# A hybrid decoder block on one core: expert blocks multiplied in pairs, and every indexed transfer an add

## The chip, the core and the metric

One core of a Trainium2 chip runs the whole program in one launch. The metric is the device time of one execution in microseconds (us). The kernel before was timed three times: 976.51, 976.25 and 974.28 us, median 976.25. One execution was profiled.

## The reference, cut to what matters

The layer takes 256 tokens of 1024 numbers. Two attention branches run side by side on the normed tokens (a block-sparse one, which with 256 tokens is plain causal attention, and a latent one), are merged by sigmoid gates, projected and added to the tokens. A channel mixer follows, and a last norm. The mixer is the part that the change touches. For each token and each of 8 heads it scores two sets of 128 sub-keys, keeps the best 16 of each, forms sums of pairs and keeps the best 16 of these. An expert is a pair of sub-keys, one of 128 x 128 = 16384. The softmax of a token's 16 best sums are its gates g, and the mixer adds up, over heads and picks,

    g * gelu(u_e . x) * v_e

where u_e and v_e are rows of two matrices of 16384 x 1024 and e is the picked expert. All of it is in float32, and the kernel has to keep that accuracy.

## The kernel before, in words

The kernel does not gather rows. It multiplies the normed tokens with all 16384 rows of u, takes the gelu of each product, multiplies these with a matrix of gates that is zero except at the picks, and multiplies the result with all rows of v. So the mixer is three streams: 16 query blocks, 128 blocks of u (128 experts each, 512 KB), 128 blocks of v.

A float32 number is kept as two parts, hi and lo, that TensorE multiplies at its fast float32 rate, and a product of two numbers is hi x hi + hi x lo + lo x hi. Each 512 KB unit of weights is loaded by SP into one of four `raw` buffers, copied into `hi` by ScalarE (L142) and subtracted into `lo` by VectorE (L146; GpSimd does this for some early units). `wget` (L155) emits the split of the units up to two ahead of the one that is used, and `emit_split` (L130) the load of the units up to three ahead of the one that it splits. There are four buffers each of `raw`, `hi` and `lo`. Every engine and every queue works in the order in which the program emits its instructions; Tile adds the semaphores.

The normed tokens stand in `h2`, for each of 8 groups of 128 channels hi and lo side by side, 256 tokens each. The first ten blocks of u, and the last four, are narrow (`u_mm`, L836): 24 products of 256 columns. Blocks 10 to 123 are wide (`u_wide`, L852): eight products of 512 columns, hi of the weight with hi and lo of the tokens at once (L857), then eight of 256, lo of the weight with hi of the tokens (L859). The sums need a PSUM bank each; blocks take two banks named `tr` and two named `sc` in twos (blocks 10 and 11 `tr`, 12 and 13 `sc`, and so on), so a bank is wanted again four blocks later.

A wide block is drained while the next one runs. `u_block` (L871) emits `u_sum` of the block before (ScalarE copies the right half, L864; VectorE adds the left half, L865), then what is handed in as `between`, then the new block's products, then `gelu_in` of the block before (L822): ScalarE writes the gelus of tokens 0 to 127 into the big buffer `gm` (L823), and those of tokens 128 to 255 into a small buffer `gs` (L828), which SP stores to the tensor `gld` in memory, one block later (`spill`, L815, L818).

The gates take two ways, one for each half of the tokens.

- Tokens 0 to 127: GpSimd writes them into a tensor `gd` of 128 x 128 x 128 zeros in memory, at addresses that each partition has in a register tile: 128 indexed transfers of 128 numbers each (`post`, L995, L1002), in eight groups of 16, one group for each head. A group may not begin before the one before it has landed. The first group writes plainly, the seven others add to what is there.
- Tokens 128 to 255: for each pair of tokens (a step q of 64) VectorE makes one-hot rows (`onehots`, L1096; L1100, L1102, two buffers each), ScalarE and VectorE weigh one set with the gates (`weigh`, L1105; L1112, L1113), TensorE multiplies them (`scatter`, L1115; two products of 256 columns, L1119), and ScalarE and VectorE put the result into `gm` (`place`, L1121; L1124, L1125). The loop at L1136 does one step with one block of u, and one block more after every third step. Step q makes the one-hots of step q + 2 and weighs those of step q + 1 (`pair`, L1132).

In the stage before that loop VectorE also finds and decodes the picks (`find`, L1016, `read`, L1026), one block of u at each yield. Between block 36 and 37 TensorE transposes the decoded indices and gates (`index_T`, L1073, `gate_T`, L1080).

After block 123 the pools of the one-hots, of `us` and of `gs` are closed (L1143 to L1146), a new pool takes their place, and SP loads gates and stored gelus back two blocks at a time (`reload`, L1156), for VectorE to multiply them into `gm` (`a_mult`, L1165), and ScalarE and VectorE to split (`a_split`, L1174). Each reload waits for the last group of indexed transfers (`ends`). The V stage then multiplies `gm` with the blocks of v: per block twelve products of 512 columns (L1194), with a scheme of fewer products for some pairs of half blocks (`w_mm`, L1270).

Of the kernel before, what the change touches and what calls it, by code (L numbers as in the profile page):

```python
# [11 lines left out]
F32 = mybir.dt.float32  # L12
# [5 lines left out]
OP = mybir.AluOpType  # L18
AX = mybir.AxisListType

P = 128
T = 256
NT = 2
D = 1024
ND = 8
# [19 lines left out]
def block_kernel(ctx, tc, consts, constb, pos, x, g_mix, g_ffn, g_fin, w_in, g_q, w_qup, g_kv, w_kvup,  # L45
                 w_ba, w_bb, w_out, w_pq, keys, exp_u, exp_v, out):
    nc = tc.nc
    V, S, G, PE = nc.vector, nc.scalar, nc.gpsimd, nc.tensor
# [6 lines left out]
    def acc():  # L55
        return ps.tile([P, 512], F32, name="acc", tag="acc", bufs=4)

    def sct():
        return ps.tile([P, 512], F32, name="sc", tag="sc", bufs=2)

    def trt():
        return ps.tile([P, 512], F32, name="tr", tag="tr", bufs=2)
# [22 lines left out]
    for dq in range(2):  # L85
        for hf in range(2):
            for u in range(2):
                k = 4 * hf + 2 * dq + u
# [66 lines left out]
    def wget(i, ahead=2):  # L155
        while state["split"] <= min(i + ahead, state["end"] - 1):
            emit_split()
        return split.pop(i)
# [14 lines left out]
    h2h, h2l = h2[:, :, 0], h2[:, :, 1]  # L173
    x2d = dram.tile([T, D], F32, name="x2d")
    gd = dram.tile([P * P * P, 1], F32, name="gd")
    gld = dram.tile([P, P, P], F32, name="gld")
# [348 lines left out]
    for hf in range(2):  # L525
        tiles = [acc(), acc()]
        hi, lo = wget(U_QUP[hf])
# [10 lines left out]
    hi, lo = wget(U_KVUP[0])  # L538
# [266 lines left out]
    gate = [gs.tile([P, 64], F32, name=f"gate{g}") for g in range(2)]  # L805
# [6 lines left out]
    T0, T1 = slice(0, P), slice(P, T)  # L812
    held = []

    def spill():  # L815
        while held:
            k, g = held.pop()
            nc.sync.dma_start(gld[k], g)  # L818

    vpool = []  # L820

    def gelu_in(j, so, keep=False):  # L822
        S.activation(gm[:, j, T0], so[:, T0], AF.Gelu)  # L823
        if keep:
            gl = vpool[0].tile([P, 2, T], F32, name="gl", tag="rl", bufs=3)[:, 0, :P]
        else:
            gl = gs.tile([P, P], F32, name="gs", bufs=3)
        S.activation(gl, so[:, T1], AF.Gelu)  # L828
        if keep:
            V.tensor_tensor(gm[:, j, T1], gm[:, j, T1], gl, op=OP.mult)  # L830
        else:
            spill()
            held.append((j, gl))


# [13 lines left out]
        gelu_in(j, u_mm(j), keep)  # L849


    def u_wide(j):  # L852
        hi, lo = wget(U_U[j])

        s = trt() if j & 2 else sct()
        for b in range(ND):
            PE.matmul(s, hi[:, b * P:(b + 1) * P], h2[:, b].rearrange("p z n -> p (z n)"), start=b == 0, stop=False)  # L857
        for b in range(ND):
            PE.matmul(s[:, :T], lo[:, b * P:(b + 1) * P], h2h[:, b, :], start=False, stop=b == ND - 1)  # L859
        return s  # L860

    def u_sum(s):
        u = gp.tile([P, T], F32, name="us", tag="us", bufs=3)
        S.activation(u, s[:, T:], AF.Copy)  # L864
        V.tensor_tensor(u, u, s[:, :T], op=OP.add)  # L865
        return u


    pend = []

    def u_block(j, keep=False, between=None):  # L871
        u = u_sum(pend[0][1]) if pend else None
        if between:
            between()
        new = j, u_wide(j)
        if pend:
            gelu_in(pend.pop()[0], u, keep)
        pend.append(new)

    def u_end(keep=False):  # L880
        j, s = pend.pop()
        gelu_in(j, u_sum(s), keep)


    qs = {}
# [109 lines left out]
    def post(g):  # L995


        for h in range(HG):
            own = []
            for k in range(16):  # L1000
                c = slice(16 * h + k, 16 * h + k + 1)
                i = nc.gpsimd.indirect_dma_start(  # L1002
                    out=gd[:, :], out_offset=bass.IndirectOffsetOnAxis(ap=addr[g][:, c], axis=0),
                    in_=gate[g][:, c], in_offset=None, compute_op=OP.add if g or h else OP.bypass).ins
                nc.gpsimd.nop()
                for m in own:
                    tc.declare_no_dep(i, m, reason="other experts")
                if k == 0:
                    for m in ends:
                        tc.add_manual_dep(i, m.name, SYNC, reason="same tokens, next head")  # L1010
                own.append(i)
            ends[:] = own
# [41 lines left out]
    done = [0]  # L1054

    def more_u(n):
        for _ in range(n):
            (u_narrow if done[0] < NP else u_block)(done[0])
            done[0] += 1
# [11 lines left out]
        more_u(1)  # L1071

    def index_T():  # L1073
        tr = trt()
        for k in range(2):
            PE.transpose(tr[:, k * P:(k + 1) * P], sel[:, k], ident)
        S.activation(ijT, tr[:, :2 * P].rearrange("p (k n) -> p k n", k=2), AF.Copy)

    def gate_T():
        tr = trt()  # L1080
        PE.transpose(tr[:, :P], sel[:, 2], ident)
        S.activation(gTh, tr[:, :P], AF.Copy)
        V.tensor_tensor(gTl, tr[:, :P], gTh.bitcast(F32), op=OP.subtract)

    more_u(1)
    index_T()
    gate_T()
    more_u(1)


    p3 = ExitStack()
    op = p3.enter_context(tc.tile_pool(name="op", bufs=2))
    NQ = P // NB
    ohi, ohj, ohw, gps = {}, {}, {}, {}

# [9 lines left out]
    def weigh(q):  # L1105

        if q < NQ:
            o = ohj.pop(q)
            ohw[q] = op.tile([P, NB, 2, P], F32R, name="ow")
            for k in range(NB):  # L1110
                t = slice(q * NB + k, q * NB + k + 1)
                S.activation(ohw[q][:, k, 0], o[:, :, k], AF.Copy, scale=gTh.bitcast(F32)[:, t])  # L1112
                V.tensor_scalar(ohw[q][:, k, 1], o[:, :, k], gTl[:, t], None, op0=OP.mult)  # L1113

    def scatter(q):  # L1115
        oi, ow = ohi.pop(q), ohw.pop(q)
        gps[q] = acc().rearrange("p (t z n) -> p t z n", t=NB, z=2)
        for k in range(NB):
            PE.matmul(gps[q][:, k], oi[:, k], ow[:, k], start=True, stop=True)  # L1119
# [12 lines left out]
    def pair(q):  # L1132
        weigh(q + 1)
        onehots(q + 2)

    for q in range(NQ):  # L1136
        scatter(q)
        u_block(done[0], between=lambda: pair(q))
        done[0] += 1
        place(q)  # L1140
        if q % 3 == 2:
            more_u(1)
    u_end()  # L1143
    spill()
    p3.close()
    pg.close()  # L1146
    NS = done[0]


    vp = ctx.enter_context(tc.tile_pool(name="vp", bufs=1))  # L1150
    vpool.append(vp)
    av, rl = {}, {}
    gview = gd.rearrange("(j i t) o -> j i (t o)", j=P, i=P)


    def reload(j):  # L1156
        if j < P:
            rl[j] = vp.tile([P, 2, T], F32, name="rl", tag="rl", bufs=3)
            i = nc.sync.dma_start(rl[j][:, :, T0], gview[j:j + 2].rearrange("j i t -> i j t")).ins
            for m in ends:  # L1160
                tc.add_manual_dep(i, m.name, SYNC, reason="gates of all heads")
            if j < NS:
                nc.sync.dma_start(rl[j][:, :, T1], gld[j:j + 2].rearrange("j i t -> i j t"))

    def a_mult(j):  # L1165
        if j in rl:
            w = T if j < NS else P
            V.tensor_tensor(gm[:, j:j + 2, :w], gm[:, j:j + 2, :w], rl.pop(j)[:, :, :w], op=OP.mult)
# [164 lines left out]
    side = []  # L1333
# [161 lines left out]
```

## Time and profile before

| | |
|---|---|
| timed runs | 976.51, 976.25, 974.28 us |
| profiled execution, its own time | 974.9 us |
| its span, first to last instruction | 973.1 us |
| TensorE busy | 959.5 us, 99% of the span |
| VectorE busy | 785.6 us, 81% |
| ScalarE busy | 598.2 us, 61% |
| GpSimd busy | 368.0 us, 38% |
| mean granted TensorE clock | 0.996 of full speed |
| from memory and to it | 189.85 MB read, 18.68 MB written |

The span is what the sums further down are made of; the profiled execution has 1.8 us around it. Busy products overlap in the trace, as TensorE starts one while the one before drains: the distance from start to start, as the chain of work shows it, is the time that a product costs.

### The profile page before, as it was taken

How to read it: one execution, taken by the hardware profiler on the slowest of the kernel's cores; microseconds unless marked ns; L12 is line 12 of the kernel's file. 1: busy time of each engine (PE TensorE's matmuls, PEld its weight loads, DVE VectorE, ACT ScalarE, POOL GpSimd, SP SyncE). 2: the span in 40 equal slices, each digit the busy share in tenths (PEclk: the TensorE clock that was granted, in tenths of full speed). 3: DMA queues.
4: the chain of work that ended last, by engine and by line, in shares of the span. 5: the costliest groups of instructions: out<-in, count | busy, mean ns of one | idle time of the engine just before them, and what ended most of it. 6: DMA issues, size and time to landing. Idle time of an engine off the chain costs nothing.

```text
span 973.1 us, 16001 instructions
## 1 busy us (share of the span) xinstructions
PE 959.5 (99%) x5237; PEld 830.1 (85%) x5238; DVE 785.6 (81%) x1704; ACT 598.2 (61%) x1191; POOL 368.0 (38%) x249
## 2 busy tenths in 40 slices
PE   9999999999998999999999999999999999999997
PEld 6878888899997888888888888988888888888885
DVE  6845347668986988888888888678999999999995
ACT  6554453543564667888887888646565665566553
POOL 7644560187727877777877820000000000000001
PEclk9999999999999999999999999999999999999999
DMA  7855457564566889888888876797777777877862
GB/s 240 292 179 164 145 195 249 175 226 164 179 201 173 204 214 214 199 196 197 199 204 204 197 197 198 231 306 264 247 257 238 262 235 251 257 239 256 258 230 80
DMA packets 126469, 209.61 MB, mean 215 GB/s; under 512 B 26881, under 2 KB 75921, under 8 KB 126258
## 3 DMA queue, kind: packets, MB, share of 16 engines
q1 hardware_dynamic: 104976, 199.14, 65.1%
q0 software_dynamic: 16896, 0.76, 5.8%
q10 hardware_dynamic: 4514, 8.68, 2.4%
q8 instruction: 42, 0.69, 0.3%
q14 instruction: 41, 0.34, 0.1%
HBM read 189.85 MB, written 18.68 MB: 214 GB/s over the span
## 4 chain that ended last, share of the span: by engine, by line
PE 95%; POOL 1%; issue 1%; DVE 1%; DMA 1%; ACT 0%; SPq 0%; another core or an unknown queue 0%; POOLq 0%; DVEq 0%
PE acc L1194 28%; PE tr L857 11%; PE sc L857 11%; PE tr L859 6%; PE sc L859 6%; PE sc L895 5%; PE acc L322 4%; PE acc L320 4%; PE acc L323 4%; PE acc L1281 3%; PE sc L1281 2%; PE tr L1281 2%; PE acc L1119 2%; PE sc L843 1%; PE sc L842 1%; PE sc L844 1%
## 5 line engine op out<-in xcount | busy, mean ns | idle before, releaser
L142 ACT ACTIVATE hi<-raw 128x1024 fp32r<-128x1024 f32 (+1 forms) x301 | 311.0, 1039 | 59.1 <-issue 22.1
L146 DVE TENSOR_TENSOR lo<-raw,hi 128x1024 fp32r<-128x1024 f32 (+2 forms) x251 | 306.2, 1223 | 50.6 <-ACT hi L142 47.7
L1002 POOL DMA_INDIRECT gd<-gate,addr x128 | 214.3, 1674 | 80.6 <-issue 58.0
L1368 POOL TENSOR_TENSOR gm<-gm 128x512 f32<-128x512 f32 x1 | 1.3, 1297 | 396.6 <-DVE gm L1364 396.6
L146 POOL TENSOR_TENSOR lo<-raw,hi 128x1024 fp32r<-128x1024 f32 x46 | 109.5, 2386 | 66.2 <-ACT hi L142 64.2
L1194 PE MATMUL acc<-lo,ah 128*128 128x512 f32 x405 | 125.0, 389 | 0.0
L1194 PE MATMUL acc<-hi,al 128*128 128x512 f32 x405 | 124.9, 389 | 0.0
L1194 PE MATMUL acc<-hi,ah 128*128 128x512 f32 x405 | 124.9, 389 | 0.0
L857 PE MATMUL tr<-h,hi 128*128 128x512 f32 x464 | 117.6, 396 | 1.6 <-issue 1.6
L857 PE MATMUL sc<-h,hi 128*128 128x512 f32 x448 | 112.3, 392 | 0.0
L857 PEld LDWEIGHTS tr<-h,hi 128*128 128x128 f32 x464 | 84.4, 191 | 16.9 <-issue 1.7
L857 PEld LDWEIGHTS sc<-h,hi 128*128 128x128 f32 x448 | 80.6, 189 | 14.4
L1194 PEld LDWEIGHTS acc<-hi,al 128*128 128x128 f32 x405 | 76.0, 188 | 15.8
L1194 PEld LDWEIGHTS acc<-lo,ah 128*128 128x128 f32 x405 | 76.0, 188 | 15.8
L1194 PEld LDWEIGHTS acc<-hi,ah 128*128 128x128 f32 x405 | 76.0, 188 | 15.6
L1171 ACT ACTIVATE ah<-gm 128x512 fp32r<-128x512 f32 x64 | 40.5, 633 | 70.0 <-PE acc L1194 41.3
L859 PEld LDWEIGHTS tr<-h,lo 128*128 128x128 f32 x464 | 63.6, 191 | 4.6
L859 PEld LDWEIGHTS sc<-h,lo 128*128 128x128 f32 x448 | 61.2, 190 | 6.0 <-issue 1.6
L859 PE MATMUL tr<-h,lo 128*128 128x256 f32 x464 | 64.9, 283 | 0.0
L859 PE MATMUL sc<-h,lo 128*128 128x256 f32 x448 | 62.8, 282 | 1.4 <-remote 1.1
L1172 DVE TENSOR_TENSOR al<-gm,ah 128x512 fp32r<-128x512 f32 x64 | 44.2, 690 | 11.7 <-ACT ah L1171 11.4
L864 ACT ACTIVATE us<-tr 128x256 f32<-128x256 f32 x58 | 22.2, 382 | 43.2 <-PE tr L859 34.2
(351 smaller groups left out, 1816.0 us busy)
## 6 DMA issues: line engine op xcount, KB each, us to landing
raw<-in_exp_u_dram SPq DMA_DIRECT2D x128, 512.0 KB
raw<-in_exp_v_dram SPq DMA_DIRECT2D x102, 512.0 KB
raw<-in_w_in_dram SPq DMA_DIRECT2D x28, 512.0 KB
gm<-in_exp_v_dram SPq DMA_DIRECT2D x52, 256.0 KB
gd<-zero ACTq DMA_DIRECT2D x8, 1024.0 KB
raw<-in_w_pq_dram SPq DMA_DIRECT2D x16, 512.0 KB
rl<-gd SPq DMA_DIRECT2D x64, 128.0 KB
gld<-gs SPq DMA_DIRECT2D x124, 64.0 KB
```

Source lines behind the costliest of these rows:

```text
L142: S.activation(hi[:, ks], r[:, ks], AF.Copy)
L146: e.tensor_tensor(lo[:, :w], r[:, :w], hi[:, :w].bitcast(F32), op=OP.subtract)
L320: PE.matmul(o, th[:, db, sl], lo[:, ws], start=False, stop=db == nd - 1)
L322: PE.matmul(o, th[:, db, sl], hi[:, ws], start=db == 0, stop=False)
L857: PE.matmul(s, hi[:, b * P:(b + 1) * P], h2[:, b].rearrange("p z n -> p (z n)"), start=b == 0, stop=False)
L859: PE.matmul(s[:, :T], lo[:, b * P:(b + 1) * P], h2h[:, b, :], start=False, stop=b == ND - 1)
L895: PE.matmul(q[:, :T], w[:, b * P:(b + 1) * P], m[:, b, :], start=k == 0 and b == 0, stop=k == 2 and b == ND - 1)
L1002: i = nc.gpsimd.indirect_dma_start(out=gd[:, :], out_offset=bass.IndirectOffsetOnAxis(ap=addr[g][:, c], axis=0), in_=gate[g][:, c], in_off ...
L1171: S.activation(h, src, AF.Copy)
L1172: V.tensor_tensor(l, src, h.bitcast(F32), op=OP.subtract)
L1194: PE.matmul(o, st[:, sl], mv[:, c:d], start=j == (0 if own is None else P - LAST) and mv is hi and st is ah, stop=j == last and st is al)
L1281: PE.matmul(o, st[a][:, ts], mv[b][:, cs], start=own and j == WJ[0] and n == 0, stop=own and j == WJ[-1] and n == 2)
```

## The change

Blocks of u go in twos. `u_wide` becomes `u_upper` (eight products of 512 columns) and `u_lower` (eight of 256 for each block whose upper products are done); an odd block runs `u_lower` for itself and the even one before it. A block is drained two blocks later in place of one, and two stand undrained at the end, so `u_end` drains two. In odd blocks the scatter products of the loop come between the products of 512 and those of 256. The transposes of indices and gates use a bank of `acc`. The one-hots' pool lies on the right side of the buffer memory, and the reload buffers get a pool `vr` of their own there, once the one-hots are closed. The stores of the last two blocks' gelus are issued by ScalarE. The first group of indexed transfers adds, as all others.

```diff
-    def spill():
+    def spill(e=None):
         while held:
             k, g = held.pop()
-            nc.sync.dma_start(gld[k], g)
+            (e or nc.sync).dma_start(gld[k], g)
...
-    def gelu_in(j, so, keep=False):
+    def gelu_in(j, so, keep=False, e=None):
...
-            spill()
+            spill(e)
             held.append((j, gl))
...
-    def u_wide(j):
+    even = []
+
+    def u_upper(j):
         hi, lo = wget(U_U[j])
         s = trt() if j & 2 else sct()
         for b in range(ND):
             PE.matmul(s, hi[:, b * P:(b + 1) * P], h2[:, b].rearrange("p z n -> p (z n)"), start=b == 0, stop=False)
-        for b in range(ND):
-            PE.matmul(s[:, :T], lo[:, b * P:(b + 1) * P], h2h[:, b, :], start=False, stop=b == ND - 1)
+        even.append((s, lo))
         return s
+
+    def u_lower():
+        while even:
+            s, lo = even.pop(0)
+            for b in range(ND):
+                PE.matmul(s[:, :T], lo[:, b * P:(b + 1) * P], h2h[:, b, :], start=False, stop=b == ND - 1)
...
-    def u_block(j, keep=False, between=None):
-        u = u_sum(pend[0][1]) if pend else None
+    def u_block(j, keep=False, between=None, among=None):
+        u = u_sum(pend[0][1]) if len(pend) > 1 else None
         if between:
             between()
-        new = j, u_wide(j)
-        if pend:
-            gelu_in(pend.pop()[0], u, keep)
+        new = j, u_upper(j)
+        if among:
+            among()
+        if j % 2:
+            u_lower()
+        if u:
+            gelu_in(pend.pop(0)[0], u, keep)
         pend.append(new)
 
     def u_end(keep=False):
-        j, s = pend.pop()
-        gelu_in(j, u_sum(s), keep)
+        assert not even
+        while pend:
+            j, s = pend.pop(0)
+            gelu_in(j, u_sum(s), keep, nc.scalar)
...
-                    in_=gate[g][:, c], in_offset=None, compute_op=OP.add if g or h else OP.bypass).ins
+                    in_=gate[g][:, c], in_offset=None, compute_op=OP.add).ins
...
     def index_T():
-        tr = trt()
+        tr = acc()
...
     def gate_T():
-        tr = trt()
+        tr = acc()
...
-    op = p3.enter_context(tc.tile_pool(name="op", bufs=2))
+    op = p3.enter_context(tc.tile_pool(name="op", bufs=2, side="right"))
...
     for q in range(NQ):
-        scatter(q)
-        u_block(done[0], between=lambda: pair(q))
+        if done[0] % 2:
+            u_block(done[0], between=lambda: pair(q), among=lambda: scatter(q))
+        else:
+            scatter(q)
+            u_block(done[0], between=lambda: pair(q))
         done[0] += 1
         place(q)
         if q % 3 == 2:
             more_u(1)
+    p3.close()
+    vr = ctx.enter_context(tc.tile_pool(name="vr", bufs=1, side="right"))
+    if done[0] % 2:
+        more_u(1)
+    spill()
     u_end()
-    spill()
-    p3.close()
+    spill(nc.scalar)
     pg.close()
...
-    vpool.append(vp)
+    vpool.append(vr)
...
-            rl[j] = vp.tile([P, 2, T], F32, name="rl", tag="rl", bufs=3)
+            rl[j] = vr.tile([P, 2, T], F32, name="rl", tag="rl", bufs=3)
```

## Rows read from the trace of the kernel before

**Rows 1.** The page, the first part (busy time of an engine, its share of the span, its instructions) and the first line of the fourth part (the chain of work that ended last, share of the span by engine).
```profile
PE 959.5 (99%) x5237; PEld 830.1 (85%) x5238; DVE 785.6 (81%) x1704; ACT 598.2 (61%) x1191; POOL 368.0 (38%) x249
...
PE 95%; POOL 1%; issue 1%; DVE 1%; DMA 1%; ACT 0%; SPq 0%; another core or an unknown queue 0%; POOLq 0%; DVEq 0%
```

**Rows 2.** The table of windows. Each row is a stretch of the span, its length, then the busy time and instructions of PE, PEld, DVE, ACT and POOL, the mean granted clock of TensorE, the DMA share and GB/s.
```profile
300.00:350.00 50.00, 46.92 (x260) 40.94 (x259) 39.48 (x81) 27.45 (x63) 40.28 (x25) 0.97 0.77 192
350.00:400.00 50.00, 50.00 (x295) 44.29 (x295) 41.86 (x92) 38.87 (x102) 35.39 (x21) 1.00 0.85 204
400.00:450.00 50.00, 50.00 (x297) 44.42 (x296) 43.20 (x98) 40.17 (x108) 39.38 (x24) 1.00 0.90 199
```

**Rows 3.** The chain that ended last, in order of time, from the first wide block of u on: start, us, what ("issue" and "an unknown queue" are idle time of TensorE for which the profile shows no releaser).
```profile
275.88 1.84 PE tr L857 x8
...
305.65 0.95 PE sc L859 x8
306.61 1.84 PE sc L857 x8
308.45 0.47 PE sc L859 x4
308.92 0.32 issue
309.24 0.28 PE sc L859
309.52 1.13 another core or an unknown queue
310.65 0.51 PE sc L859 x3
311.16 1.64 issue
312.80 3.43 PE tr L857 x8
316.23 1.08 PE tr L859 x8
317.31 1.84 PE tr L857 x8
```

**Rows 4.** Around 310 us: three rows of the timeline (start, us, engine, line, operation, what it writes and reads; in brackets the idle time of the engine before it and what ended that), then a row of the table of windows.
```profile
309.91 0.96 POOL L1002 DMA_INDIRECT gd<-gate,addr  x1 [0.30 <-issue]
...
310.73 0.39 ACT L864 ACTIVATE us<-tr 128x256 f32<-128x256 f32 x1 [7.75 <-remote]
...
311.15 0.42 DVE L865 TENSOR_TENSOR us<-us,tr 128x256 f32<-128x256 f32 x1 [5.13 <-issue]
...
312.80:316.40 3.60, 3.60 (x10) 2.86 (x10) 1.55 (x3) 1.97 (x6) 3.15 (x2) 0.53 0.52 158
```

**Rows 5.** The timeline of GpSimd: the indexed transfers that begin the first, the second and the third group of sixteen, and the last transfer.
```profile
288.55 1.59 POOL L1002 DMA_INDIRECT gd<-gate,addr  x1 [17.40 <-ACT gm L823]
...
312.95 1.87 POOL L1002 DMA_INDIRECT gd<-gate,addr  x1 [2.08 <-issue]
...
353.76 1.56 POOL L1002 DMA_INDIRECT gd<-gate,addr  x1 [4.39 <-issue]
...
564.43 1.56 POOL L1002 DMA_INDIRECT gd<-gate,addr  x1 [0.30 <-issue]
```

**Rows 6.** The chain in order of time, in two stages with products of one width: a query block (256 columns) and a stretch of the V stage (512 columns).
```profile
200.17 2.87 PE sc L895 x24
...
680.40 16.32 PE acc L1194 x72
```

**Rows 7.** The end of the blocks of u: the timeline of SP's stores, of the first narrow product of block 124 and of VectorE's lower half for block 126, and from the chain the first products of the V stage.
```profile
609.99 0.38 SPq L818 DMA_DIRECT2D gld<-gs  x1
...
612.45 4.51 SPq L818 DMA_DIRECT2D gld<-gs  x3
...
614.97 0.28 PE L842 MATMUL sc<-h,hi 128*128 128x256 f32 x1
...
617.59 1.23 DVE L146 TENSOR_TENSOR lo<-raw,hi 128x1024 fp32r<-128x1024 f32 x1 [1.52 <-ACT hi L142]
...
626.65 48.99 PE acc L1194 x216
```

**Rows 8.** The stage that decodes the picks: a row of the table of windows, and from the timeline one block's sum, ScalarE's copy and VectorE's add.
```profile
346.00:352.00 6.00, 6.00 (x35) 5.27 (x34) 5.73 (x13) 3.88 (x9) 3.06 (x2) 1.00 0.93 231
...
284.30 0.38 ACT L864 ACTIVATE us<-sc 128x256 f32<-128x256 f32 x1 [0.31 <-PE sc L859]
...
287.62 0.42 DVE L865 TENSOR_TENSOR us<-us,sc 128x256 f32<-128x256 f32 x1
```

**Rows 9.** The timeline of one steady block of the loop with its scatter: TensorE's 512s, and of VectorE the sum, the last one-hot, the lower half and the placing; and, from the chain in order of time, the two scatter products of a later block.
```profile
421.88 2.00 PE L857 MATMUL tr<-h,hi 128*128 128x512 f32 x8
...
422.32 0.42 DVE L865 TENSOR_TENSOR us<-us,tr 128x256 f32<-128x256 f32 x1 [0.61 <-ACT us L864]
...
423.25 0.42 DVE L1102 TENSOR_TENSOR oi<-ijT,iota 128x256 fp32r<-128x256 bf16 x1
...
423.85 1.23 DVE L146 TENSOR_TENSOR lo<-raw,hi 128x1024 fp32r<-128x1024 f32 x1 [0.18 <-ACT hi L142]
...
424.99 0.43 DVE L1125 TENSOR_TENSOR gm<-gm,acc 128x256 f32<-128x256 f32 x1
...
433.70 0.24 PE acc L1119 x2
```

More of the change, by code (lines that the diff above doesn't have):

```diff
@@ L1142, in block_kernel @@
             more_u(1)
+    p3.close()
[3 more added lines that the diff above has]
+    spill()
     u_end()
-    spill()
-    p3.close()
+    spill(nc.scalar)
     pg.close()
     NS = done[0]
+    assert NS % 2 == 0
     vp = ctx.enter_context(tc.tile_pool(name="vp", bufs=1))
-    vpool.append(vp)
+    vpool.append(vr)
     av, rl = {}, {}
```

## The prediction

> **What bounds the kernel now.** I began with the page. TensorE is busy for 99% of the span and holds 95% of the chain that ended last, VectorE for 81% [rows 1]. So the time is the sum of what TensorE's products take, plus what little it waits, and an edit is worth what it takes off that one engine. The table of windows says where it waits: of the 50 us from 300 to 350 it is busy for 46.92 at a mean clock of 0.97, in the windows after that for 50.00 of 50.00 at 1.00 [rows 2]. One stretch can give something back; elsewhere only shorter products can.
>
> The chain in order of time has both. A U block is eight products of 512 columns (1.84 us) and eight of 256 (0.95 us) [rows 3]. The eleven blocks from 275.88 to 306.61 took 30.73 us, 2.794 each [rows 3]. From 308.92 the same rows show a hole: idle, one product, idle, three products, idle, and then a block of 512 in 3.43 us in place of 1.84. The block that began at 306.61 and its successor should have ended at 306.61 + 2 x 2.794 = 312.20; the next began at 317.31. **The hole costs 5.11 us**: some 3.1 of it idle [rows 3], the rest a clock that fell from 2.4 to 1.2 GHz after the idle time (granted 0.53 from 312.80 to 316.40) [rows 4].
>
> What the engines did in the hole: ScalarE waited 7.75 us for a block's sum, VectorE 5.13 us behind it, and TensorE stopped in the middle of a row of eight products whose operands were there. Nobody was busy but GpSimd, which was issuing the last of its first sixteen indexed transfers [rows 4]. These sixteen, from 288.55 to 309.91, are the only ones that write plainly; the 112 after them add [rows 4, 5]. TensorE ran again at 310.65 and ScalarE at 310.73, while the last plain one was being issued.
>
> **The change part by part.**
>
> *Pairs.* In the V stage 72 products of 512 take 16.32 us, 0.2267 each, and in the query stage 24 of 256 take 2.87, 0.1196 each [rows 6]. Eight and eight of these are 2.770 us; a block takes 2.794. The 0.024 us over is what changing between the widths costs (the eight of 512 take 1.84 where 1.814 would do). A pair changes once where two blocks changed twice, so it saves 0.024 us; blocks 10 to 123 make 57 pairs: **-1.35 us**. It can't be under nothing, as no product is added, nor over 57 x 0.048 = 2.7, with every change gone. I take 1.35, which the difference itself gives.
>
> [...]
>
> *The adds.* With an add in place of the plain write the first sixteen transfers become like the others. A plain round lasts from 288.55 to 312.95 (24.4 us), a round of adds from 312.95 to 353.76 (40.8), the next being shorter. So GpSimd's last transfer moves from 564.43 to at most 581 [rows 5]. Who waits for it is the first reload, which isn't issued before 612 [rows 7]: 31 us of cover, so nothing. The gain is the hole, if it belongs to the plain writes: while adds run, TensorE is busy for 50.00 us of 50 [rows 2]. No row shows a plain transfer without the hole's neighbourhood, so the term lies between 0 and -5.11. I take **-5.11**: the hole lies inside the plain round, ends with it, is the only one, and 112 adds have none.
>
> *The added waits.* First, sums come later: a block's 256-column products wait for its partner's 512s, and its PSUM bank is wanted again four blocks on. An even block's bank used to be drained from the block after it, with three blocks (8.4 us) to spare; now from the pair's end, with two (5.6 us). The worst pressure is in the stage that decodes the keys, where VectorE is busy for 5.73 us of 6 [rows 8]. There a sum copied by ScalarE at 284.30 was added by VectorE only at 287.62, 2.9 us after the copy ended [rows 8]. 2.9 is under 5.6: nothing; were the cover gone, each pair would pay the excess.
>
> Second, in odd blocks the scatter products move behind the eight of 512, while the one-hots for two rounds later, which take the same buffer, are still issued ahead of them. VectorE's L1102 therefore waits for a scatter that now comes 1.84 us later. Queued behind it are the lower half of a later weight (L146, 1.23 us), the add of the placed columns (L1125) and the next block's sum. In a steady block of 3.03 us VectorE's work runs from 422.32 to 425.4 [rows 9]. Reckoned over a pair, with both scatters, of 6.04 us: the even block's VectorE work ends some 2.5 us after the pair's start, the odd block's one-hot starts at 4.3 (twice 1.84 and 0.24 [rows 9], and the drain), the lower half ends at 5.9 and the add at 6.3, a fifth of a microsecond into the next pair, where the slack catches it. That lower half is first read 4 us later. Nothing on the path.
>
> *The end of U.* Two sums are pending in place of one, and the stores of the last two gelus go from SP's queue to ScalarE's. SP sat 4.51 us on three such stores, and the reloads and V's weights queued behind them [rows 7]. They move up, but TensorE ran from the narrow blocks into V at 626.65 without a hole, so this gains at most the 0.2 us by which four narrow blocks (96 x 0.1196 = 11.48) miss the 11.68 between 614.97 and 626.65 [rows 7]. ScalarE gets a copy and two gelus more before its next split, about 0.8 us, and two issues of 0.4 to 1.5 us (0.38 for a free one, 4.51/3) [rows 7]. The lower half of block 126, ready at 618.82 [rows 7], is wanted at 620.8. It would be ready at 620.4 or, with the long issues, at 622.6. I take 0, as most issues are near the short end, and keep 0 to +1.8 for the range. The transposes of the indices take a bank of the scatter's four, which nothing uses before block 39, and the reload buffers over the one-hots wait for the last scatter in place of the last gelu; both end earlier than they are wanted, so nothing.
>
> Sum: -5.11 - 1.35 = **-6.46 us**. The profiled execution took 974.9 us (span 973.1 and 1.8 around it), so 968.4. The median shown is 976.25, 1.35 above it, by which it would be 969.8; what spreads the three runs over 2.2 us no row tells. I forecast **969.2**.
>
> **The rivals.** What counts as no change is 0.3%, 2.9 us, about what a measurement of this kernel can tell.
>
> *A, as above* (0.56): 967 to 971.5.
>
> *B, the hole stays* (0.23). For it: TensorE ran undisturbed through the first 20 us of plain writes, up to 308.92, and a wait for "remote" or "issue" may be anything that stops all engines, at one moment of one trace; the profiler's own traffic could be part of it, in which case the timed runs have nothing to lose. Against it: the coincidence at both ends, and a profiled time (974.9) no longer than the others. Only the pairs count: 974.9 - 1.35 = 973.5, by the median 974.9. No change. The Trainium skill's "DMA: Bandwidth & Descriptors", section "Specifications", speaks for this one: it says that a transfer of under 512 B is a read-modify-write in any case, so that an add would load the memory like a plain write. No run here shows that yet.
>
> *C, the order of the products costs nothing* (0.10), the hole goes all the same: what looks like a change of width would be a fixed cost of a new bank or of its signal, paid per block in either order. Then -5.11 alone: 969.8, by the median 971.1. Faster still. [...]
>
> *D, slower* (0.09): VectorE falls behind in the decoding stage, blocks 10 to 36, 13 pairs. Its price is what the lag exceeds 5.6 us by, per pair; at 95% busy it has 0.25 us in 5.6 to recover with. The gains are spent at 6.46/13 = 0.5 us a pair, and slower by over 0.3% begins at 0.7. At 1 us it gives 974.9 - 6.46 + 13 = 981.4. Against it: a lag of 2.9 measured.
>
> The 0.02 left is a hole that shrinks by half: 971 to 972.3.
>
> **How the numbers follow.** Faster are A, C and the half hole, 0.68; no change is B, 0.23; slower is D, 0.09. The range: below, 966.5 (A from the fastest run, 974.28 - 6.46 = 967.8, and the other half of the width changes, 1.35); above it has to reach over B, 974.9, and some of the end's 1.8: 975.5. It leaves out D and little else. For the faster cases alone it would be 966.5 to 972.
>
> **What would show it.** Right: no idle TensorE in the decoding stage and a granted clock of 1.00 from 300 to 350; sixteen of 512 in about 3.65 us and sixteen of 256 in 1.91, a pair in 5.56; a first round of transfers of 37 to 41 us; the end of U without a hole. Wrong: a hole of microseconds in the first round of adds (B), a wait of the first 512 on VectorE's add (D), 5.59 a pair (C), or a split late before block 126.

## The result, and the profile after

The kernel after took 969.52 us (median of four runs, 969.34 to 970.09); the kernel before, run beside it, 976.38 (974.28 to 977.10). The ratio is 0.9937, with a 95% interval of 0.9925 to 0.9950: faster by 6.9 us, where 969.2 us was forecast. The profiled execution took 969.34 us with a span of 967.5, 5.6 less than before.

The page after, its first part and the chain by engine, beside [rows 1]:

```profile
PE 956.7 (99%) x5237; PEld 828.4 (86%) x5238; DVE 781.1 (81%) x1704; ACT 598.7 (62%) x1191; POOL 373.0 (39%) x249
...
PE 94%; POOL 2%; DVE 1%; issue 1%; ACT 1%; DMA 0%; POOLq 0%; DVEq 0%; ACTq 0%
```

TensorE still bounds the kernel. What it lost is in the windows of 50 us, beside [rows 2] (columns: stretch, its length, then busy time and instructions of TensorE, its weight loads, VectorE, ScalarE, GpSimd, then granted clock, DMA share, GB/s):

```profile
300.00:350.00 50.00, 50.00 (x289) 44.23 (x288) 43.30 (x87) 30.68 (x71) 40.03 (x23) 1.00 0.90 214
```

From 300 to 350, where it had been busy for 46.92 at a clock of 0.97, it is now busy throughout at 1.00. The chain of work in order of time (start, duration, what), beside [rows 3]:

```profile
276.47 3.65 PE tr L860 x16
280.12 1.91 PE tr L868 x16
282.04 3.65 PE sc L860 x16
...
332.14 3.65 PE tr L860 x16
...
621.02 19.07 PE acc L1217 x84
```

Ten pairs from 276.47 to 332.14 take 5.567 us each; two blocks took 5.588. From the first wide block to the first product of V the kernel after takes 621.02 - 276.47 = 344.55, the kernel before 626.65 - 275.88 = 350.77 [rows 3, 7]: 6.22 less. The stages ahead took 0.59 longer, the rest the same, which gives the 5.6.

GpSimd's transfers, beside [rows 5]: the first of the first round, of the second round, and the last.

```profile
288.44 2.20 POOL L1016 DMA_INDIRECT gd<-gate,addr  x1 [16.70 <-ACT gm L823]
...
327.46 1.55 POOL L1016 DMA_INDIRECT gd<-gate,addr  x1 [3.31 <-issue]
...
569.94 1.55 POOL L1016 DMA_INDIRECT gd<-gate,addr  x1 [0.30 <-issue]
```

The first round lasts 39.0 us in place of 24.4; the last transfer ends at 571.5.

### The profile page after: what moved, and what is told of

It is laid out like the page before. It is cut to its first block, busy times and chain, and to the rows that moved or that the text cites. A ratio compares the mean times of both kernels' runs of the same rounds, so it can differ in the third digit from the quotient of the medians.

```text
span 967.5 us, 15965 instructions
## 1 busy us (share of the span) xinstructions
PE 956.7 (99%) x5237; PEld 828.4 (86%) x5238; DVE 781.1 (81%) x1704; ACT 598.7 (62%) x1191; POOL 373.0 (39%) x249
## 4 chain that ended last, share of the span: by engine, by line
PE 94%; POOL 2%; DVE 1%; issue 1%; ACT 1%; DMA 0%; POOLq 0%; DVEq 0%; ACTq 0%
PE acc L1217 28%; PE tr L860 11%; PE sc L860 11%; PE tr L868 6%; PE sc L868 6%; PE sc L909 5%; PE acc L320 3%; PE acc L322 3%; PE acc L323 3%; PE acc L1304 3%; PE sc L1304 2%; PE tr L1304 2%; PE acc L1133 2%; PE sc L843 1%; PE sc L842 1%; PE sc L844 1%
## 5 line engine op out<-in xcount | busy, mean ns | idle before, releaser
L142 ACT ACTIVATE hi<-raw 128x1024 fp32r<-128x1024 f32 (+1 forms) x301 | 311.1, 1040 | 58.8 <-issue 20.7
L1016 POOL DMA_INDIRECT gd<-gate,addr x128 | 218.6, 1708 | 81.2 <-issue 58.9
L860 PE MATMUL tr<-h,hi 128*128 128x512 f32 x464 | 110.7, 391 | 0.0
L860 PE MATMUL sc<-h,hi 128*128 128x512 f32 x448 | 107.2, 391 | 0.0
L868 PE MATMUL tr<-h,lo 128*128 128x256 f32 x464 | 60.2, 283 | 0.0
L868 PEld LDWEIGHTS tr<-h,lo 128*128 128x128 f32 x464 | 58.0, 191 | 0.5
L868 PE MATMUL sc<-h,lo 128*128 128x256 f32 x448 | 58.1, 283 | 0.0
L868 PEld LDWEIGHTS sc<-h,lo 128*128 128x128 f32 x448 | 56.0, 191 | 0.5
L1116 DVE TENSOR_TENSOR oi<-ijT,iota 128x256 fp32r<-128x256 bf16 x64 | 27.3, 426 | 34.6 <-PE acc L1133 34.6
```

The lines of the kernel that those rows point to most:

```text
L142: S.activation(hi[:, ks], r[:, ks], AF.Copy)
L1016: i = nc.gpsimd.indirect_dma_start(out=gd[:, :], out_offset=bass.IndirectOffsetOnAxis(ap=addr[g][:, c], axis=0), in_=gate[g][:, c], in_off ...
```

## The experiments

Two theories stood at the start. A: the hole of [rows 3] belongs to the plain writes and the adds remove it; the pairs are worth about 1.35 us beside it. Its rivals: the hole has another cause, or the pairs' order of products is worth nothing. The kernel before ran again beside each set: 975.18 us for the first four runs, 972.86 for e5, e6, e8 and e9, 972.77 for the last four. Below, "freeze" is the time in which ScalarE and VectorE stand still at "remote" or "issue" while GpSimd writes, and "hole" what TensorE loses by it; a "pair" is two blocks of u in the order of the change, a "single block" one in the order of before.

**e1, the pairs with the plain first round.**

```diff
-    in_=gate[g][:, c], in_offset=None, compute_op=OP.add).ins
+    in_=gate[g][:, c], in_offset=None, compute_op=OP.add if g or h else OP.bypass).ins
```

> The changed kernel with one thing undone: the first sixteen indexed transfers write plainly again. Theory A (the hole belongs to the plain writes): a hole returns between some 303 and 317 us, TensorE idle there for about 3 us and the granted clock down for one stretch of 3.4 us; the time goes from 969.5 to about 974.6, 5.1 up. Theory B (the hole is something else, and went for another reason: the new order of products, or chance): no hole, 969.5 within 1 us. If the timed runs are up by 5 and not only the profiled one, the hole is no product of profiling.

969.75 us (969.55 to 970.06), ratio to before 0.9945 (0.9928 to 0.9961). A miss: as fast as the kernel after. Yet the freeze is there. ScalarE's first work after it, with the idle time ahead in brackets:

```profile
313.96 0.39 ACT L872 ACTIVATE us<-sc 128x256 f32<-128x256 f32 x1 [5.67 <-remote]
```

The chain on TensorE beside it:

```profile
308.37 1.91 PE sc L868 x16
310.28 3.20 PE tr L860 x14
313.53 0.72 PE tr L860 x2
```

ScalarE waits 5.67 us, the last 3.68 of them for a sum that was complete when its pair ended, at 310.28; TensorE loses 0.06 (310.28 + 3.20 is 313.48). So the pairs without the adds remove the hole too.

**e2, the adds with the single blocks of before.**

```diff
-    in_=gate[g][:, c], in_offset=None, compute_op=OP.add if g or h else OP.bypass).ins
+    in_=gate[g][:, c], in_offset=None, compute_op=OP.add).ins
```

> The kernel before with one edit: all indexed transfers add. Theory A: no hole from 300 to 350, TensorE busy for 50.00 us there, 976.3 - 5.1 = 971.2. Theory B: the hole stays, 976.3. What is left to the changed kernel's 969.5 is what the pairs bring: 1.35 forecast, a block 2.794 us against half a pair 2.782; by theory C (order costs nothing) 0.

970.31 us (969.77 to 970.53), ratio 0.9949 (0.9933 to 0.9966). Its window from 300 to 350:

```profile
300.00:350.00 50.00, 50.00 (x289) 44.02 (x288) 43.90 (x86) 31.44 (x73) 39.40 (x22) 1.00 0.89 215
```

No hole. The chain has the first wide block and the first product of V:

```profile
276.55 1.84 PE tr L857 x8
...
622.20 17.93 PE acc L1194 x79
```

From the one to the other it takes 345.65 us: 5.12 less than before, the hole's 5.11; the pairs take off the 1.10 that is left to 344.55. Here the freeze itself is gone: from 300 to 320 no wait of ScalarE is longer than 1.2 us. In time, across the first two sets, the pairs are worth 0.8 us with the adds there (970.31 to 969.52), and the adds 0.2 with the pairs there (969.75 to 969.52). The two edits overlap.

**e3, the widths alternating from product to product** (the pairs' sums and drains as in the kernel after).

```diff
         for b in range(ND):
             PE.matmul(s, hi[:, b * P:(b + 1) * P], h2[:, b].rearrange("p z n -> p (z n)"), start=b == 0, stop=False)
-        even.append((s, lo))
+            PE.matmul(s[:, :T], lo[:, b * P:(b + 1) * P], h2h[:, b, :], start=False, stop=b == ND - 1)
         return s
```

> The changed kernel with the widths changing at every product: 512, 256, 512, 256 and so on, eight times in a block in place of once in two. If each change to and fro costs 0.024 us, as the prediction has it, a block takes 2.770 + 8 x 0.024 = 2.96 us, 0.18 more than in the changed kernel, and 114 blocks 20 us more: 989. If the order costs nothing (theory C: a fixed cost per block), 2.78 a block and 969.5. A number between the two would say that the cost is in a longer row of 512s after 256s and not in each change.

974.27 us (973.56 to 974.50), 4.8 above the kernel after: between the two forecasts. The order does cost, so rival C falls, but not a fixed 0.024 us at each change. That the cost lies in a longer row of 512s, which the expectation made of such a number, was not tried by itself. The chain has two blocks from 421.70 to 427.35:

```profile
421.70 0.23 PE sc L860
421.93 0.12 PE sc L861
...
427.35 0.24 PE acc L1133 x2
```

2.825 us a block, 0.055 above the 2.770 of the products by themselves, with eight pairs of changes; one pair of changes cost 0.024 in a block of before. Over 114 blocks, 2.825 against 5.567/2 makes 4.7 us, which is the time measured.

**e4, all 128 transfers plain**, on the pairs.

```diff
-    in_=gate[g][:, c], in_offset=None, compute_op=OP.add).ins
+    in_=gate[g][:, c], in_offset=None, compute_op=OP.bypass).ins
```

> The changed kernel with all 128 indexed transfers plain, eight groups of sixteen (where a token picks one expert in two heads, the later gate replaces the earlier one in place of being added to it). Theory A as a dose: a hole near the end of each group while blocks of u run, eight of some 5 us, so up to 40 us more: about 1010; GpSimd's groups of 24 us in place of 36. If a hole needs what else goes on in the decoding stage (VectorE at 95%), then only the groups in that stage have one: 5 to 15 us more, 975 to 985. Theory B: 969.5.

1001.51 us (994.53 to 1004.49), ratio 1.0247 (1.0207 to 1.0287). TensorE loses time near the end of five of the eight groups (idle for 3.5, 4.6, 5.4, 1.9 and 4.6 us in the second, third, fifth, sixth and eighth); when the transfers are over, it loses none. A window with a hole, and one behind the last transfer:

```profile
355.00:365.00 10.00, 5.57 (x21) 3.93 (x20) 2.54 (x4) 3.56 (x9) 5.38 (x5) 0.71 0.21 59
500.00:550.00 50.00, 50.00 (x292) 44.80 (x293) 42.76 (x100) 41.75 (x111) 0.00 (x0) 0.97 0.65 202
```

TensorE's products in that hole, and ScalarE's row there (start, duration, engine, line, idle time ahead):

```profile
358.80 0.28 PE L868 MATMUL tr<-h,lo 128*128 128x256 f32 x1 [0.31 <-issue]
360.22 0.37 PE L868 MATMUL tr<-h,lo 128*128 128x256 f32 x1 [1.14 <-issue]
361.66 0.37 PE L868 MATMUL tr<-h,lo 128*128 128x256 f32 x1 [1.07 <-issue]
...
358.18 0.38 ACT L872 ACTIVATE us<-sc 128x256 f32<-128x256 f32 x1 [8.84 <-remote]
```

The plain writes make the freeze: further groups bring more of it. And the pairs do not always ride through: in the first group they did, as in e1 (ScalarE waited 5.60 us, TensorE nothing), in five others TensorE gave out single products, some more than a microsecond apart. The ends of the two groups that are left, the fourth and the seventh:

```profile
385.00:394.00 9.00, 9.00 (x57) 8.07 (x56) 7.26 (x20) 6.72 (x19) 4.65 (x5) 1.00 0.75 209
466.00:476.00 10.00, 10.00 (x61) 8.87 (x60) 8.24 (x21) 7.84 (x22) 5.84 (x5) 1.00 0.76 202
```

There was nothing to ride through: no wait of ScalarE in these groups is longer than 1.2 us. They are also the two whose writes followed each other slowest, 1.61 and 1.82 us from one to the next on average, against 1.32 to 1.52 in the six others. The holes differ from the one of e13 below: TensorE waited at "issue", inside rows of products, and for no split of weights. Its largest line in the table of waits (in total, times, longest):

```profile
PE tr L868 <- issue: 14.4, 20, 1.7
```

The next question was what in the plain writes does it.

**e5, all plain, in groups of eight** (the edit against e4).

```diff
+                if k == 8:
+                    ends[:] = own
+                    own = []
...
-                if k == 0:
+                if k in (0, 8):
                     for m in ends:
                         tc.add_manual_dep(i, m.name, SYNC, ...)
```

> The kernel after with all 128 indexed transfers writing plainly, as in the run with all of them plain (1001.5 us), but in 16 groups of eight, each waiting until the eight before it have landed. Where a token picks one expert in two heads, the later gate replaces the earlier one. Theory 1: the freeze needs a long run of plain writes that are under way together; in that run it came after 12 to 14 of 16 in a group, so groups of eight are free of it, and the time is that of the kernel after, 969 to 971.5 us, with TensorE busy for 50.00 us in every window of 50 from 300 to 550. Theory 2: every plain write adds to the freeze, however they are grouped: 1001 us again, holes in the second half of U.

970.61 us (968.75 to 972.91): theory 1, but for a remainder. The windows are full except these two, which lack 0.6 and 0.9 us:

```profile
450.00:500.00 50.00, 49.42 (x288) 43.43 (x288) 42.47 (x97) 40.52 (x108) 31.34 (x26) 1.00 0.68 195
500.00:550.00 50.00, 49.10 (x288) 43.55 (x287) 40.40 (x96) 39.16 (x103) 23.53 (x23) 1.00 0.69 196
```

Both stops come right behind the two eights that were issued fastest (from 451.48 to 460.32 and from 511.75 to 520.61, 1.26 us from one write to the next); the fourteen others took 1.33 or more on average and cost nothing. So the pace of the writes counts beside their number.

**e6, the kernel before with its first, plain group cut in two eights** (the same edit, for that group alone).

> The kernel before, its first sixteen transfers still plain, but the ninth waits until the eight before it have landed; nothing else differs. Theory 1 (a long run is needed): no hole, 970.3 us, as the kernel before with nothing but adds. Theory 2 (any plain write does it): 975.2 us, a hole of about 5 us at the end of the group.

970.34 us (970.16 to 970.78), ratio 0.9972 (0.9961 to 0.9983). The transfers about the cut:

```profile
300.61 0.96 POOL L1005 DMA_INDIRECT gd<-gate,addr  x1 [0.31 <-issue]
305.54 1.24 POOL L1005 DMA_INDIRECT gd<-gate,addr  x1 [3.96 <-issue]
```

Its window from 300 to 350:

```profile
300.00:350.00 50.00, 50.00 (x288) 44.02 (x287) 43.41 (x86) 31.52 (x73) 35.84 (x23) 1.00 0.79 212
```

One wait of 3.96 us on GpSimd after the eighth write, and single blocks with plain writes have no hole.

**e8, all plain in sixteens, spaced by memsets** (the edit against e4; the buffer that they write, and the room made for it, are left out).

```diff
+                for _ in range(10):
+                    G.memset(dly, 0.0)
```

> The kernel after with all transfers plain in groups of sixteen (1001.5 us), and ten small memsets of GpSimd behind each transfer, so that a plain one follows the last at about the distance of an add (1.9 us in place of 1.3). The later gate of a token's twofold expert replaces the earlier. Rate theory: GpSimd issues plain writes faster than they are finished, adds no faster than they are, so that spaced plain writes leave no freeze: 969 to 972 us. Kind theory: it is the plain write itself, at any spacing: over 990 us, holes at the ends of groups.

1038.87 us (1038.35 to 1039.46): the time lies where the kind theory put it, over 990 us, but for another reason; the trace has none of its holes and agrees with the rate theory. Its window from 300 to 350:

```profile
300.00:350.00 50.00, 50.00 (x290) 44.17 (x289) 43.22 (x87) 30.66 (x71) 37.55 (x174) 1.00 0.74 216
```

TensorE's longest wait, by the table of waits (in total, times, longest), and then the longest of SP's queue from 600 to 720:

```profile
PE acc L1220 <- ACT hi L142: 66.5, 1, 66.5
```

```profile
SPq L1185 <- DMA gd<-gate,addr: 75.3, 2, 55.9
```

TensorE is busy for 50.00 of 50 in all windows from 300 to 600: plain writes at 2.8 us or more from each other make no hole, sixteen or not. The memsets spaced them wider than the 1.9 us that was meant, GpSimd ended its last transfer at 681 in place of 571, and V's first reload waited for it. So this run also shows what stands behind the cover that the prediction put on GpSimd: once it is used up, TensorE pays, 66.5 us here.

**e9, the kernel before with its plain round to come later**: fourteen memsets ahead of the first transfer.

> The kernel before, with fourteen small memsets of GpSimd ahead of its first indexed transfer, so that the whole round of plain writes moves by 1 to 2 us against the blocks of U; nothing else differs. Theory of the phase: the freeze of the other engines comes every time, but what TensorE loses by it depends on where in a block it strikes, as the pairs rode through one of 4.6 us with nothing lost. Then the hole is smaller or gone: anything from 970 to 975. Theory of the fixed hole: the single blocks always lose 5 us to it: 975.2 us.

973.15 us (972.61 to 975.35), ratio 1.0002. The try failed as a shift: the memsets ran in GpSimd's idle time before the first transfer, which began 12.68 us after the first wide block (289.04 and 276.36), as before (12.67). As a second look at the kernel before it is of use. Its chain:

```profile
297.75 0.97 PE sc L860 x8
...
317.71 1.84 PE sc L858 x8
```

Between 298.72 and 317.71 lie six blocks, 18.99 us in place of 16.76. The hole is 2.2 us here and 5.1 in the first profile, at the same place.

**e13, the same with nine memsets behind the first transfer.**

```diff
+                if not (g or h or k):
+                    for _ in range(9):
+                        G.memset(dly, 0.0)
```

> The kernel before, with nine small memsets of GpSimd (some 1.5 us) between its first and second indexed transfer, so that the fifteen other plain ones, still at 1.27 us from each other, move by half a block of U. (In the earlier try the memsets ran in GpSimd's idle time ahead of the first transfer, and moved nothing.) Theory of the phase: the hole is of another size by more than 1.5 us, up or down, than in the runs of the kernel before beside it. Rival: the hole's size has nothing to do with where in a block the freeze strikes: within 1 us of the kernel before.

976.78 us (974.81 to 977.45), ratio 1.0037 (1.0023 to 1.0051): 4.0 us more, with the last plain write 1.3 us later (22.62 us behind the first in place of 21.36). The rows show a part of what TensorE lacked. ScalarE first:

```profile
310.62 0.38 ACT L865 ACTIVATE us<-tr 128x256 f32<-128x256 f32 x1 [6.77 <-PE sc L858]
310.89 1.05 ACT L142 ACTIVATE hi<-raw 128x1024 fp32r<-128x1024 f32 x1
```

TensorE in the same stretch:

```profile
309.15 0.99 PE L860 MATMUL sc<-h,lo 128*128 128x256 f32 x7
310.57 0.35 PE L860 MATMUL sc<-h,lo 128*128 128x256 f32 x1 [0.43 <-issue]
312.00 0.98 PE L858 MATMUL tr<-h,hi 128*128 128x512 f32 x3 [1.07 <-ACT hi L142]
313.40 0.40 PE L858 MATMUL tr<-h,hi 128*128 128x512 f32 x1 [0.42 <-issue]
```

And two pieces of the chain, the starts of the blocks before and behind:

```profile
304.68 1.84 PE sc L858 x8
...
317.64 1.82 PE tr L858 x8
```

The product at 312.00 waits for a split of weights (L142) that stood in ScalarE's queue behind the copy of a sum (L865), and the copy waited for its signal through the freeze. In the program's order the copy of block j - 1 and the split for block j + 2 follow each other. The copy can start when block j does, here at 304.68 by the chain; the split's products are wanted two blocks (5.59 us) later, at 310.27. Copy and split take 1.32 us, so a copy that is late by over 4.3 us holds TensorE up. This one was 5.94 late; the products came at 312.00, 1.73 late. The row puts 1.07 us of that down to the split; a stop of 0.43 at "issue", one product earlier, had come first. The hole is 4.6 us in all (two blocks from 307.47 to 317.64); the rest is further stops inside a row of products, at "issue", and a lower clock.

**e12, single blocks that are drained two blocks later**, with the plain first round.

```diff
     new = j, u_upper(j)
...
-        if j % 2:
-            u_lower()
+        u_lower()
```

> The kernel after with the first sixteen transfers plain (969.75 us), and with every block's eight products of 256 right behind its eight of 512, as in the kernel before; sums are still drained two blocks later. Theory of the later drain: that TensorE rode through the freeze with nothing lost comes from the sums that are wanted later; then nothing but the changes of width are paid, 57 x 0.02 = 1.1 us: 970.5 to 971.3. Theory of the pairs: it comes from the pairs themselves, and the hole is back: 972.5 to 975.

970.48 us (969.73 to 970.89): the later drain. From 300 to 350 TensorE is busy for 50.00. The order of the products is that of before; the later drain, the one difference in this stretch, is what took the hole away. Here the copy of block j - 2 stands ahead of the split for block j + 2: three blocks, 8.4 us, from the one's signal to the other's use. But this trace does not show that slack at work, as the freeze was shorter:

```profile
309.60 0.39 ACT L872 ACTIVATE us<-sc 128x256 f32<-128x256 f32 x1 [2.70 <-remote]
```

The sum had been complete at 306.50, so its copy was 3.1 us late, which is under the 4.3 that single blocks can bear. Whether a later drain bears a longer freeze, or makes for a shorter one, is not shown.

**e14, e1 with the memsets of e13.**

> The kernel after with the first sixteen transfers plain (969.75 us), the fifteen behind the first moved in the same way by 1.5 us, a quarter of a pair. Theory of the phase: that the pairs lost nothing was an accident of where the freeze struck; here a hole shows, 971 to 975 us. Rival: the pairs ride through wherever it strikes: 969.3 to 970.3.

969.19 us (969.18 to 969.43): as the kernel after. ScalarE's first work after the freeze:

```profile
313.24 0.39 ACT L873 ACTIVATE us<-sc 128x256 f32<-128x256 f32 x1 [5.51 <-remote]
313.52 1.05 ACT L142 ACTIVATE hi<-raw 128x1024 fp32r<-128x1024 f32 x1
```

The chain on TensorE:

```profile
307.81 1.91 PE sc L869 x16
309.72 3.65 PE tr L861 x16
313.37 1.91 PE tr L869 x16
315.28 3.64 PE sc L861 x16
```

Windows of 2 us in the freeze:

```profile
310.00:312.00 2.00, 2.00 (x10) 1.65 (x9) 0.17 (x2) 0.00 (x0) 1.68 (x2) 1.00 0.80 235
312.00:314.00 2.00, 2.00 (x14) 1.77 (x13) 0.34 (x1) 0.76 (x2) 0.95 (x1) 1.00 0.16 40
```

A pair's sums are both complete when the pair ends, at 309.72 here; the copy came 3.5 us after, its split was done at 314.57, and the next pair wanted it at 315.28: 0.7 us to spare. The windows say that the engines stop before the data does: from 310 to 312 the DMA engines still moved 235 GB/s, while ScalarE, whose sum was complete, did nothing and VectorE next to nothing. That the signals are what is held up is a reading of these rows; an engine that lacked its next instruction would look the same, and no run tells the two apart.

**e7, the last gelus' stores by SP**, as before.

```diff
-            gelu_in(j, u_sum(s), keep, nc.scalar)
+            gelu_in(j, u_sum(s), keep)
...
-    spill(nc.scalar)
+    spill()
```

> The kernel after, with the stores of the last two blocks' gelus issued by SP, as before, in place of ScalarE. Theory of the prediction: the end of U waits for none of this, 969.5 us, TensorE without idle time from 600 to 640. Rival: the reloads queue behind stores that sit in SP's queue for 1.5 us each, V starts later by 1 to 3 us: 970.5 to 972.5.

969.47 us (969.02 to 970.05): no difference, as forecast. TensorE is busy for 40.00 of 40 from 600 to 640 in both.

## Why the prediction was right, point by point

**What bounds the kernel.** Right: one hole and the products' own time were all there was to gain. The 6.22 us that the blocks of u lost are 5.12 and 1.10.

**Pairs, -1.35.** The mechanism held (e3: the order costs), the size was a little over: 1.10 in the traces, 0.8 between the timed runs. The step that was off is "A pair changes once where two blocks changed twice, so it saves 0.024 us": a pair takes 5.567, still 0.027 above the 5.540 of its products, with 0.048 in two single blocks and 0.110 in two alternating ones. No one price for a change fits these three. The Trainium skill's "TensorE: Matmul & The Clock Gate", section "Back-to-back issue gap", gives the distance of products in a stream by their columns alone, about 131 ns at 512. Here it was 226.7 ns [rows 6], and e3's 4.8 us show that their order has a price as well.

**Adds, -5.11.** The forecast term was measured at 5.12 (e2, against the same trace of before), and B falls: seven more plain groups of sixteen bring more holes (e4), none of the kernels with adds alone has one. Two things in the step were not as told. First, "if it belongs to the plain writes" is too wide: eight at a time they make none (e6) or next to none (0.6 and 0.9 us in e5), and at 2.8 us from each other sixteen make none (e8). It takes a run of them at a quick pace; in e4 groups of sixteen at 1.61 and 1.82 us made none either. Second, the term was not the adds' alone: the edits' gains were summed as if independent, and e1 shows that the other edits give the same 5 us without the adds. The sum came out right because the adds were counted for the hole once and the pairs not for it. The adds are the safer of the two: with plain groups all through, the pairs lost some 32 us (e4), and with adds there is nothing to ride through.

**Why TensorE stopped.** The prediction noted that it stopped "in the middle of a row of eight products whose operands were there". That was part of it. What it did not follow is ScalarE's queue: in e13 1.1 of the 4.6 us are a wait for a split of weights that stood behind a sum's copy. The added wait that was costed at nothing (sums drained a block later) was looked at for its PSUM bank alone; for ScalarE's queue the same delay is slack, from two blocks to three in e12. In pairs it is two blocks again, but a pair's end comes only every 5.57 us, and in e1 and e14 it fell late in the freeze: the copy was 3.7 and 3.5 us late, in e13 5.9. That the later drain cures the hole is shown (e12); that it does so by this slack is argued. It does not explain e4, whose holes are stops at "issue". What stops TensorE inside a row stays open, and so does the step by which the writes hold up the engines.

**The spread of before.** The prediction said that no row tells what spreads its runs over 2.2 us. The record points to the hole: 5.1 and 2.2 us in two traces at the same place (before and e9, whose executions took 974.9 and 973.0), and medians of 976.4, 975.2, 972.9 and 972.8 in four sets. Kernels without a hole stayed where they were from set to set, though the last three sets ran on three different chips: the kernel after and e7, its twin in time, at 969.5 in the first and the last, e2 and e6, single blocks both, at 970.3 in the second and the third. The gain is thus 6.9 us in the set of the result and 3.3 in the last (e7's ratio is 0.9964, 0.9951 to 0.9976). That the forecast met the first has some luck in it: its 5.11 was read from one execution with a large hole, and between e6 and its set the hole was worth 2.5.

**Costed at nothing.** GpSimd's last transfer ended at 571.5, under the 581 of the prediction, and the cover is real (e8). The end of U: nothing (e7). The one-hots' wait for a scatter did appear on VectorE and cost nothing, as TensorE stayed at 50.00 of 50. In the kernel after, all idle time of VectorE ahead of L1116:

```profile
DVE oi L1116 <- PE acc L1133: 34.6, 41, 1.3
```

**D, slower.** It did not come: no product waits for a sum's add.

**The rule that spoke for B.** An add is not like a plain write to the memory in these traces. The page's row of GpSimd's queue (packets, MB, share) after, with 128 adds:

```profile
q0 software_dynamic: 18688, 0.76, 6.4%
```

and in e4, with 128 plain writes:

```profile
q0 software_dynamic: 4352, 0.76, 0.6%
```

146 packets for an add, 34 for a plain write. That a write of under 512 B is a read-modify-write in any case (Trainium skill, "DMA: Bandwidth & Descriptors", "Specifications") did not make the two alike. It is the lighter one, issued faster, that brings the freeze.

## What to carry to other kernels

When every engine but one stops for "remote" or "issue", look at what the one is issuing: here a wait after eight of its writes, or an add in their place, took the same hole away as a new order of the products with its later drains. Two edits that may cure the same hole are to be tried one at a time before their gains are summed. And the slack of a delayed drain is counted in the draining engine's whole queue, not only in the bank that it empties: what stands behind the drain may be what the bottleneck needs next.

## What the runs showed of the hardware that was not expected

- In runs of sixteen plain indexed writes from GpSimd, mostly at 1.3 us from one to the next, the other engines stood still for several us (ScalarE waited 2.7 to 8.8 in all of them but the sixth group of e4), with data still moving in part of that time (235 GB/s).
- The same writes at a slower pace (two groups of e4 at 1.61 and 1.82 us on average, e8 at 2.8), or as adds with four times the packets, did not do this; in eights TensorE lost 0.9 us at most behind one (e5, e6).
- Alternating products of 512 and 256 columns take 0.353 us for the two, 0.007 above the same products in rows of a kind.
